# Sliding windows by DMA: one more staged batch, and all direct copies as halves

## The chip, the core and the metric

The kernel runs on one core of a Trainium2 chip. It has no arithmetic at all: it is a program of DMA transfers, which 16 DMA engines carry out. Three of the core's instruction streams issue transfers, and each has a ring (queue) of its own on those engines: SP (SyncE), ACT (ScalarE) and POOL (GpSimd). The metric is the device time of one execution in microseconds (us); lower is better.

## The reference

The input x has 32 batches of 4096 rows of 256 float32. The output holds, for each batch, 127 windows of 64 rows each, which start every 32 rows, so each window shares half of its rows with the next one.

```python
batch, length, dim = (32, 4096, 256)      # window_size 64, stride 32
n_windows = (length - window_size) // stride + 1
for i in range(n_windows):
    start = i * stride
    result[:, i] = x[:, start:start + window_size].copy()
```

A block here is 32 rows of one batch, 32 KB. A batch has 128 blocks (4 MB, 4.19 million bytes); window w is block w followed by block w + 1, 64 KB, and the output of a batch is 8.32 million bytes. All of it is 266 MB.

## The kernel before

There are two ways in which a batch gets to the output.

**Direct.** `Copier.windows` copies n windows from x in HBM to the output in HBM. With `half=None` a row is a whole window of 64 KB (two packets of 32 KB, the largest piece, DIRECT). With `half=0` or `half=1` a row is only the first or the second block of each window (32 KB, one packet), written with a gap of 32 KB, so that two DMAs, a pair, do the same as one full DMA. The usual DMA covers 16 windows (a "sixteen"), one row for each of the 16 engines.

**Staged.** Every third batch (1, 4, 7, ... 31; 11 of them) goes through on-chip memory. `Staging.load` brings the 128 blocks of a batch into a tile of 128 partitions with 32 KB each; `Staging.store` writes the tile out twice, once as the first halves of the windows and once as the second halves. Packets are 16 KB here (IN and OUT). Six tiles are used in turn: `Staging.run` loads six batches, stores six, loads the other five, and stores those. All of this is issued by ACT; before a tile is loaded again, ACT waits for its stores, and before it is stored, for its load. The very first load and the very last store are cut into smaller DMAs. The staged stores write 128 rows although a batch has 127 windows, so each spills one wrong half window into the batch before it (its last window, 126) and one into the batch after it (its window 0). These have to be written again later, after the store.

The direct batches' 127 windows are cut into 7 sixteens, which leaves 15 over: the edges. Beside a staged batch the edges lie at the side of that batch, so that they cover the spilled half window: windows 0 to 14 where the batch before is staged, 112 to 126 where the batch after it is. With two direct batches in each gap between staged ones, each direct batch has one staged neighbour.

**The order.** SP issues the 147 sixteens, batch by batch (the loop from line 174), and one small DMA in the middle for a last half window. For each sixteen a running sum, `share`, decides whether it goes as one full DMA or as a pair of halves: pairs take 90 of 120 while ACT's ring loads, 18 of 120 while it stores, and all of the first 16 turns (and those about the start of the second loads). The counters `first_loads`, `loads` and `stores` estimate from the turns passed which of the two ACT's ring is at. The last but one sixteen counts on the semaphore `near`.

POOL waits for `near` (line 193 on), then issues the edges, batch by batch. Before each it waits until the stores of the staged neighbours are done (`wait_stored`). The edges of all but batch 30, the last direct one, are 20 DMAs of 15 windows; 4 more windows of batch 30 bring them to 304, a multiple of 16. `columns`, also on POOL, brings the next 9 windows of batch 30 in pieces of 4 KB, 16 for each half. SP at last waits for the first stores of tile 31 and then copies the last two windows of batch 30 with `columns`, and waits for everything.

Of the kernel before, what the change touches and what calls it, by code (L numbers as in the profile page):

```python
# [125 lines left out]
@with_exitstack  # L126
def kernel(
    ctx: ExitStack,
    tc: tile.TileContext,
    x: bass.AP,  # L130
    window_size: bass.AP,
    stride: bass.AP,
    out: bass.AP,
):
    nc = tc.nc
    W, S = int(window_size), int(stride)
    B, L, D = x.shape
    n_win = (L - W) // S + 1
    assert out.shape == (B, n_win, W, D)
    c = Copier(x, out, B, L, D, W, S, n_win)  # L140


    staged = [*range(1, B, 3)]
    items = [(b, -1 if b == B - 1 else 0, c.nb) for b in staged]
    place = {b: g for g, (b, _, n) in enumerate(items) if n == c.nb}
    direct = [b for b in range(B) if b not in staged]
    pool = ctx.enter_context(tc.tile_pool(name="xb", bufs=1))
    st = Staging(c, tc, pool, x.dtype, items, 6)
    ring_d, ring_s, ring_r = nc.sync, nc.scalar, nc.gpsimd
    done = tc.alloc_semaphore("done")  # L150
    near = tc.alloc_semaphore("near")
    rest = tc.alloc_semaphore("rest")
    total = {done: 0, near: 0, rest: 0}

    def count(dma, sem):
        dma.then_inc(sem, 16)
        total[sem] += 16

    sixteens = []
    for b in direct:
        w = 15 if b - 1 in staged else 0
        sixteens += [(b, w + 16 * j) for j in range((c.nw - w) // 16)]
    singles = [(B - 1, c.nw - 1, 1)]
    edges = [(b, 0 if b - 1 in staged else 112, 15) for b in direct[:-1]]
    last = B - 2
    edges.append((last, 112, 4))

    first_loads, loads, stores = 6 * 17, 5 * 17, 6 * 34  # L170
    turns = share = 0
    with tc.tile_critical():  # L172
        st.run(ring_s)

        for i, (b, w) in enumerate(sixteens):
            sem = near if i == len(sixteens) - 2 else done
            second = turns - first_loads - stores
            loading = turns < first_loads or 0 <= second < loads
            share += 120 if turns < 16 or -8 <= second < 16 else 90 if loading else 18
            if share >= 120:  # L180
                share -= 120
                turns += 4
                count(c.windows(ring_d, b, w, 16, 0), done)
                count(c.windows(ring_d, b, w, 16, 1), sem)
            else:
                turns += 3
                count(c.windows(ring_d, b, w, 16), sem)
            if i == len(sixteens) // 2:
                for b, w, half in singles:
                    count(c.windows(ring_d, b, w, 1, half, 2048), done)  # L190

        ring_r.wait_ge(near, 16)
        for b, w, n in edges:
            for k in (b - 1, b + 1):
                if k in place and b != last:
                    st.wait_stored(ring_r, place[k])
            count(c.windows(ring_r, b, w, n), rest)


        count(c.columns(ring_r, last, 116, 9), rest)  # L200
        ring_r.drain()  # L201
        st.wait_stored(ring_d, place[B - 1])
        count(c.columns(ring_d, last, 125, 2), done)
        total[st.ended] = st.count[st.ended]
        for sem, n in total.items():
            ring_d.wait_ge(sem, n)
# [35 lines left out]
```

## Time and profile before

| what | us |
|---|---|
| median of 3 runs | 753.65 |
| lowest, highest run | 752.89, 753.98 |
| span of the profiled execution, first to last instruction | 742.1 |
| median of the runs less that span | 11.55 |
| last packet of SP's sixteens ends, from the span's start | 651.4 |
| last packet of ACT's stores ends | 738.9 |
| last packet of POOL's ring ends | 739.7 |

The page gives the span in 40 slices of 18.55 us, with the share of the 16 DMA engines that was busy (in tenths) and what they moved in each. Under it stand the queues: q1 is SP's ring, q10 is ACT's and q0 is POOL's, with packets, MB, and the time of those packets as a share of what 16 engines have in the span. Packets overlap a little, so a share can come out slightly over 1. A DMA's completion is a packet of 4 bytes on each engine that took part. The time between a DMA's issue and its landing is long here (about 100 us on the median for SP's), because many are queued ahead.

### The profile page before, as it was taken

How to read it: one execution, taken by the hardware profiler on the slowest of the kernel's cores; microseconds unless marked ns; L12 is line 12 of the kernel's file. 1: busy time of each engine (PE TensorE's matmuls, PEld its weight loads, DVE VectorE, ACT ScalarE, POOL GpSimd, SP SyncE). 2: the span in 40 equal slices, each digit the busy share in tenths (PEclk: the TensorE clock that was granted, in tenths of full speed). 3: DMA queues.
4: the chain of work that ended last, by engine and by line, in shares of the span. 5: the costliest groups of instructions: out<-in, count | busy, mean ns of one | idle time of the engine just before them, and what ended most of it. 6: DMA issues, size and time to landing. Idle time of an engine off the chain costs nothing.

```text
span 742.1 us, 323 instructions
## 1 busy us (share of the span) xinstructions
POOL 12.7 (2%) x26
## 2 busy tenths in 40 slices
POOL 0000000000000000000000000000000000050100
DMA  8999999999999999999999999999999999999996
GB/s 361 424 430 427 435 431 428 423 435 425 428 427 426 428 428 420 429 435 427 427 427 412 433 435 431 427 436 432 434 424 429 430 424 426 428 435 432 421 420 253
DMA packets 18290, 313.26 MB, mean 422 GB/s; under 512 B 4336, under 2 KB 4336, under 8 KB 4528
## 3 DMA queue, kind: packets, MB, share of 16 engines
q1 hardware_dynamic: 8016, 154.32, 48.8%
q10 hardware_dynamic: 9104, 138.41, 44.0%
q0 software_dynamic: 1168, 20.51, 6.6%
q14 instruction: 2, 0.02, 0.0%
HBM read 220.95 MB, written 267.09 MB: 658 GB/s over the span
## 4 chain that ended last, share of the span: by engine, by line
another core or an unknown queue 92%; POOL 2%; issue 0%; POOLq 0%; SPq 0%
POOL out_dram L34 2%; POOLq L201 0%; POOLq L237 0%; SPq L172 0%; POOLq L114 0%
## 5 line engine op out<-in xcount | busy, mean ns | idle before, releaser
L34 POOL DMA_DIRECT2D out_dram<-in_x_dram x21 | 12.0, 575 | 685.4 <-DMA out_dram<-in_x_dram 648.7
L44 POOL DMA_DIRECT2D out_dram<-in_x_dram x1 | 0.6, 581 | 0.0
L223 POOL MEMSET const-float32-0.0<- 128x1 f32 x1 | 0.1, 98 | 0.2 <-issue 0.2
L223 POOL MEMSET const-bfloat16-1.0<- 128x1 bf16 x1 | 0.1, 101 | 0.0
L223 POOL MEMSET const-float32-1.0<- 128x1 f32 x1 | 0.1, 98 | 0.0
L223 POOL MEMSET const-uint8-127<- 128x1 uint8 x1 | 0.1, 98 | 0.0
## 6 DMA issues: line engine op xcount, KB each, us to landing
out_dram<-in_x_dram SPq DMA_DIRECT2D x92, 1024.0 KB, 99.8
out_dram<-xb ACTq DMA_DIRECT2D x21, 4096.0 KB, 138.5
out_dram<-in_x_dram SPq DMA_DIRECT2D x110, 512.0 KB, 90.2
xb<-in_x_dram ACTq DMA_DIRECT2D x10, 4096.0 KB, 130.5
out_dram<-in_x_dram POOLq DMA_DIRECT2D x20, 960.0 KB, 37.9
xb<-in_x_dram ACTq DMA_DIRECT2D x4, 1024.0 KB, 15.7
out_dram<-xb ACTq DMA_DIRECT2D x2, 1024.0 KB, 110.5
out_dram<-xb ACTq DMA_DIRECT2D x4, 512.0 KB, 94.4
```

Source lines behind the costliest of these rows:

```text
L34: return q.dma_start(out=self.oap((b * self.nw + w0) * 2 + h, [[2 * blk, n], row]), in_=self.xap(b * self.nb + w0 + h, [[blk, n], row]), m ...
L44: return q.dma_start(out=self.oap((b * self.nw + w0) * 2, [[part, 16], [2 * self.blk, n], row]), in_=self.xap(b * self.nb + w0, [[part, 16 ...
L223: nc = _bacc.Bacc("TRN2", target_bir_lowering=False, num_devices=1)
```

## The change

Batches 18 and 20 are staged in place of 19, so that 12 of 32 are staged and three gaps (17, 19, 21) hold one direct batch, with a staged one at either side; the other gaps hold two as before. ACT's ring has two equal groups of six loads and six stores. The edges of a batch with two staged neighbours are cut in two, 7 windows at its start and 8 at its end, and each of the two waits for both neighbours. The number of windows of batch 30 that go with the edges is worked out from their sum (`odd`, 3 here), and `columns` takes the 10 that follow. The running sum with its turns is gone: each sixteen is a pair of halves.

```diff
-    staged = [*range(1, B, 3)]
+    staged = [1, 4, 7, 10, 13, 16, 18, 20, 22, 25, 28, B - 1]
...
-    sixteens = []
+    sixteens, edges = [], []
+    last = B - 2
     for b in direct:
-        w = 15 if b - 1 in staged else 0
-        sixteens += [(b, w + 16 * j) for j in range((c.nw - w) // 16)]
+        first = (15 if b + 1 not in staged else 7) if b - 1 in staged else 0
+        sixteens += [(b, first + 16 * j) for j in range((c.nw - first) // 16)]
+        if b != last:
+            edges += [(b, w, n) for w, n in ((0, first), (first + 112, 15 - first)) if n]
     singles = [(B - 1, c.nw - 1, 1)]
-    edges = [(b, 0 if b - 1 in staged else 112, 15) for b in direct[:-1]]
-    last = B - 2
-    edges.append((last, 112, 4))
-
-    first_loads, loads, stores = 6 * 17, 5 * 17, 6 * 34
-    turns = share = 0
+    odd = -sum(n for _, _, n in edges) % 16
+    edges.append((last, 112, odd))
+
     with tc.tile_critical():
         st.run(ring_s)
 
         for i, (b, w) in enumerate(sixteens):
-            sem = near if i == len(sixteens) - 2 else done
-            second = turns - first_loads - stores
-            loading = turns < first_loads or 0 <= second < loads
-            share += 120 if turns < 16 or -8 <= second < 16 else 90 if loading else 18
-            if share >= 120:
-                share -= 120
-                turns += 4
-                count(c.windows(ring_d, b, w, 16, 0), done)
-                count(c.windows(ring_d, b, w, 16, 1), sem)
-            else:
-                turns += 3
-                count(c.windows(ring_d, b, w, 16), sem)
+            count(c.windows(ring_d, b, w, 16, 0), done)
+            count(c.windows(ring_d, b, w, 16, 1), near if i == len(sixteens) - 2 else done)
...
-        count(c.columns(ring_r, last, 116, 9), rest)
+        count(c.columns(ring_r, last, 112 + odd, 13 - odd), rest)
```

## The prediction

> **What bounds the kernel now.** I read the page's slices first, to see whether the transfers ever pause; then its queue table, for what a byte costs on each ring; then the busy time by stretch; then the waits. No compute engine does anything here, so everything is DMA.
>
> The first view is the page: the span, its 40 slices and the queues.
>
> ```profile
> span 742.1 us, 323 instructions
> ...
> DMA  8999999999999999999999999999999999999996
> GB/s 361 424 430 427 435 431 428 423 435 425 428 427 426 428 428 420 429 435 427 427 427 412 433 435 431 427 436 432 434 424 429 430 424 426 428 435 432 421 420 253
> ...
> q1 hardware_dynamic: 8016, 154.32, 48.8%
> q10 hardware_dynamic: 9104, 138.41, 44.0%
> q0 software_dynamic: 1168, 20.51, 6.6%
> ...
> HBM read 220.95 MB, written 267.09 MB: 658 GB/s over the span
> ```
>
> q1 is SP's ring (direct copies), q10 ACT's (staged loads and stores), q0 POOL's (edges). The three shares add to 99.4% of sixteen engines' span. Only the first and the last slice are not full, so there is no gap to fill: the time is the sum of what the packets cost. The second view gives the rate by stretch (start to end in us, length, POOL busy, clock, DMA share, GB/s).
>
> ```profile
> 0.00:20.00 20.00, 0.20 (x4) 1.00 0.90 367
> 20.00:125.00 105.00, 0.00 (x0) 1.00 1.01 429
> 140.00:400.00 260.00, 0.00 (x0) 1.00 1.00 428
> 420.00:510.00 90.00, 0.00 (x0) 1.00 1.01 433
> 545.00:645.00 100.00, 0.00 (x0) 1.00 1.01 428
> 655.00:735.00 80.00, 6.66 (x12) 1.00 1.00 421
> 735.00:742.00 7.00, 0.00 (x0) 1.00 0.10 40
> ```
>
> The reader sees one ceiling, 428 to 433 GB/s, whether ACT's ring loads (20 to 125, 420 to 510) or stores (140 to 400, 545 to 645). In the trace's packet records the commonest 32 KB direct packet takes 1213 ns and the commonest 16 KB staged packet 611 ns, in every stretch; the means are 1223 and 618 ns, so some packets are drawn out, by 0.8 and 1.1%. A resource that runs against its ceiling in nine tenths of its packets is the engines' own rate. So I ask first how many bytes the change makes them move.
>
> **What the change does to the bytes.** Batch 19 becomes direct, 18 and 20 become staged: 12 staged batches and 20 direct ones. A direct batch moves its 127 windows of 64 KB once, 8.32 MB. A staged one moves 4.19 MB in and twice 4.19 MB out, 138.41 / 11 = 12.58 MB. By ring:
> - q10: 12 x 12.58 = 150.99 MB (+12.58).
> - q1: all 20 direct batches have 7 sixteens (112 windows), 140 in place of 147, each 1.049 MB: 154.32 - 7.34 = 146.98 MB.
> - q0: edges fall from 304 windows to 288 (19 batches x 15, and 3 of batch 30), columns rise from 9 to 10: 298 x 65.5 KB = 19.53 MB (-0.98).
> Together 317.50 MB against 313.24, or +4.26 MB.
>
> Each ring's price comes from its share: q1 0.488 x 742.1 = 362.1 us for 154.32 MB, 2.347 us a MB; q10 326.5 / 138.41 = 2.359; q0 49.0 / 20.51 = 2.388. After: 146.98 x 2.347 = 344.9, 150.99 x 2.359 = 356.2, 19.53 x 2.388 = 46.6; sum 747.7 us against 737.6. **The extra staged batch costs +10.1 us.**
>
> **All direct DMAs as halves.** 92 of 147 sixteens are now full (one DMA of 1 MB); all 140 become pairs of 512 KB. SP issues 280 DMAs of sixteens instead of 202. The data packets stay 32 KB. What grows is one completion packet on each of the 16 engines per DMA, which the packet records show at 9 ns: 78 x 9 ns = 0.7 us, **+0.8 us** with the part that the price per MB had already taken off. The issuing itself is hidden: SP's shortest issue takes 558 ns, 280 of them 156 us in a ring that works over 670 us, and its median DMA lands some 90 to 100 us after its issue, so SP is far ahead. If that lead were gone, each issue would show up at half a microsecond.
>
> A rule speaks against halves here. The Trainium skill, page "DMA: Bandwidth & Descriptors", section "Rules for kernel authors", asks for at least 1 MiB a DMA, and its section "Anatomy of one DMA — SWDGE (gpsimd) path" puts about 2 us fixed on each of POOL's; laid end to end, 78 more DMAs would be an estimated 156 us by that page. The rows above show the engines at share 1.00 in stretches with three quarters halves, so that fixed part lies under other DMAs.
>
> **The pace of the two rings.** The code counts turns: a full is 3 (two packets and a completion), a pair 4, a staged tile 17 (16 packets and a completion), and the engines alternate between rings. The third view, the queues of 545 to 645 us (packets, MB, share), tests it:
>
> ```profile
> q1 hardware_dynamic: 1191, 24.55, 57.7%
> ...
> q10 hardware_dynamic: 1188, 18.22, 43.0%
> ```
>
> As many packets on one ring as on the other. So the order of the end can be forecast. Between them, a pair on q1 and four turns on q10 cost 2 x 1.222 + 4 x 0.576 = 4.75 us, a full and three turns 4.16 us. Before: 92 x 4.16 + 55 x 4.75 = 644 us; the trace ends q1's sixteens at 651.4, 7.5 later (ramp and slow packets). After: 140 x 4.75 + 7.5 = 672 us. Turns on q10: before 10 x 17 + 20 loading, 20 x 17 + 39 storing, 569, so some 71 were left when q1 ended; after 620, less 562, some 60. q0 answers with 69 turns before (38 data packets, 21 + 1 completions, 9 columns) and 70 after (36, 23 + 1, 10). **The two rings still end within 2 or 3 us of each other**, and one ring alone does not starve the engines: from 650 to 655 us, before q0's packets came, nearly all was q10 at 432 GB/s. I cost the new balance at 0, bounds -2 and +3.
>
> **Waits.** The fourth view is what POOL waited for (us, times, longest).
>
> ```profile
> POOL out_dram L34 <- DMA out_dram<-in_x_dram: 648.7, 1, 648.7
> POOL out_dram L34 <- DMA out_dram<-xb: 36.8, 1, 36.8
> ```
>
> The first is `near`, the second the staged store of batch 28, ahead of the edges of 27 and 29. Edges of batches 17, 19 and 21 now come in two (7 and 8 windows), each with waits for both neighbours; tiles 5 to 8 are stored well before 672 us, so these pass at once, for three more issues of 0.57 us on POOL. Again only the edges of 27 and 29 will wait, for batch 28 (21 turns left at 562, about 27 us). Queued behind them on POOL are the 3 windows of batch 30 and the columns. Ahead of them on q0 lie 255 windows, 16.7 MB, which at q0's 246 GB/s (8.62 MB between 660 and 695 us) last 68 us. Cost 0; if that cover were gone, up to 27 us. SP's last wait, for the last tile, stays as it is.
>
> **Slow packets.** The unknown: do 12 tiles and halves everywhere change the drawn-out packets? Stretches with three quarters halves (the code's 90 of 120; 20 to 125 and 400 to 510) average 429.6 GB/s, store stretches with 15% (18 of 120; 140 to 400 and 510 to 645) about 428.1. That is 0.35% of some 485 us of storing (24 stores x 17 turns x 1.187 us), -1.7 us, which I take, since the halved stretches are the nearest rows. Ends: all packets at their commonest time, 0.8% of 362 and 1.1% of 326 us and q0's, -7 us; and the slowest 20 us ahead of the tail, 416 GB/s (400 to 420 us), through all storing, 2.8%, +14 us. The ramp at the start and the thin 7 us at the end are the same code: 0, +-3.
>
> **Sum:** 10.1 + 0.8 - 1.7 = +9.2 us. Profiled span 742.1 + 9.2 = 751.3; the runs' median is 11.5 us above the span (753.65), so **762.8 us**, +1.2%.
>
> **Rivals.**
> - **Slow packets vanish** in storing, as from 420 to 540 us, where 432 GB/s held: 10.9 - 7 = +3.9, 757.6 us. For it: less is read from HBM at a time, as q1's part falls from 57 to about 52%. Against it: in the first loads, with 75% halves, they did not vanish.
> - **HBM decides (faster).** A direct batch reads and writes HBM 16.64 MB, a staged one 12.58: HBM bytes fall by about 4.1 MB. If the 658 GB/s over the span were the limit, that is -6.2 us, 747.5 us. Its condition is that slices with less HBM traffic per byte moved move more. Against it: 140 to 400 us has q1 at 63.48 of 111.19 MB and 428 GB/s, 80 to 120 us q1 at 9.11 of 17.29 and 432: 0.9% apart while HBM traffic differs by 2.9%; and a 32 KB packet cannot fall below the 1213 ns it has when nothing presses. It decides only if the drawn-out share of packet time exceeds the 10.9 us added; it is about 7.
> - **Halves collide in storing.** Both rings would write only every second 32 KB at once. Load stretches with halves have just one such writer. Price half to all of the bound above: 10.9 + 7 to 14, 771.6 to 778.6 us. For it: the edges' last part, 700 to 735, falls to 407 GB/s with other writers mixed. Against: ACT's stores have that pitch already.
> - That the change does not do what it says (the rings end apart) costs little, as shown: inside the forecast's range.
>
> **Chances.** Forecast 0.66 (759.5 to 768), slow packets vanish 0.16 (754 to 759.5), halves collide 0.13, HBM 0.05. A difference under 0.2% (1.5 us) can't be told from none: faster 0.05, same 0.04 (the low end of the second case), slower 0.91. The range leaves out HBM's case, the low edge of the second and most of the third: 756.5 to 768.
>
> **What would show it.** Right: q10 near 151 MB, q1 near 147, engines at 9 to the last slice, mean GB/s again 421 to 425 over a span of 750 to 753, q1's sixteens ending near 672, POOL's second wait under 40 us, commonest packets still 1213 and 611 ns. Wrong: a steady rate of 432 or more in storing (second case), under 422 (third), or a last slice emptier than 253 GB/s (the balance).

## The result, and the profile after

The changed kernel takes 756.38 us (median of 8 runs, 755.60 to 757.53); the kernel before, beside it, 754.11 us (8 runs, 752.89 to 754.59). The ratio is 1.0032, 95% interval 1.0019 to 1.0045: slower by 2.3 us. I had forecast 762.8, with a range from 756.5. The sign was right, the size was four times too large.

One number must be read before the profile. The changed kernel's profiled execution took 756.57 us and its span is 754.8: **only 1.8 us lie outside the span.** The recorded profile of the kernel before spans 742.1, so that execution took about 744 us, while all eight timed runs took 753 to 755. The two spans are 12.7 us apart, the medians 2.3.

The page of the changed kernel: span, the DMA slices, and the queues (packets, MB, share).

```profile
span 754.8 us, 412 instructions
...
DMA  8999999999999999999999999999999999999995
GB/s 359 423 427 429 431 431 431 431 431 430 432 430 432 432 432 431 431 437 431 414 430 429 432 435 431 434 430 431 431 431 426 431 432 433 431 438 424 411 389 178
...
q10 hardware_dynamic: 9920, 151.00, 47.0%
q1 hardware_dynamic: 9040, 146.98, 45.5%
q0 software_dynamic: 1280, 19.53, 6.6%
...
HBM read 216.83 MB, written 267.16 MB: 641 GB/s over the span
```

The bytes are those worked out: 151, 147 and 19.5 MB. The slices are different from those of before: 24 of the 40 stand at 430 to 432, where they had wavered between 412 and 436, and the last three are thinner (178 GB/s in the last, where 253 had been seen before). The same in stretches of the changed kernel (start to end, length, POOL busy, clock, DMA share, GB/s):

```profile
140.00:400.00 260.00, 0.00 (x0) 1.00 1.01 430
520.00:660.00 140.00, 0.00 (x0) 1.00 1.01 431
675.00:735.00 60.00, 4.69 (x9) 1.00 1.01 411
735.00:754.00 19.00, 0.00 (x0) 1.00 0.56 191
```

SP's sixteens end at 669.7 us (672 forecast). ACT's last packet ends at 742.6 us and POOL's at 752.4; before, these two rings ended within a microsecond of each other. From 728 to 742 us POOL's copies are nearly alone (packets, MB, share; 4.83 MB in all, 345 GB/s):

```profile
q0 software_dynamic: 241, 4.56, 94.5%
q10 hardware_dynamic: 26, 0.21, 4.2%
```

POOL's waits:

```profile
POOL out_dram L34 <- DMA out_dram<-in_x_dram: 665.8, 1, 665.8
POOL out_dram L34 <- DMA out_dram<-xb: 20.0, 1, 20.0
```

The second is the wait for batch 28, 20.0 us where 27 was worked out, and the new pairs of waits cost nothing, as forecast.

To compare kernels I use one measure from the packet records, the **drawn-out time**: what each packet took over the commonest time of its size (1213 ns for 32 KB, 611 for 16 KB, 159 for 4 KB), summed and divided by 16 engines. In the recorded trace of before it is 7.6 us, 5.9 of it until SP's sixteens end and 1.7 behind; in the changed kernel's 7.9 us, 2.7 until then and 5.2 behind. POOL's 32 KB packets there average 1320 ns.

### The profile page after: what moved, and what is told of

Its sections match the earlier page's. It is cut to its first block, busy times and chain, and to the rows that moved or that the text cites. A ratio compares the mean times of both kernels' runs of the same rounds, so it can differ in the third digit from the quotient of the medians.

```text
span 754.8 us, 412 instructions
## 1 busy us (share of the span) xinstructions
POOL 13.6 (2%) x28
## 4 chain that ended last, share of the span: by engine, by line
another core or an unknown queue 91%; POOL 1%; issue 0%; POOLq 0%; SPq 0%
POOL out_dram L34 1%; POOLq L191 0%; POOLq L227 0%; SPq L172 0%; POOLq L114 0%
```

## The experiments

Eight runs were made on one chip (the first chip, below), where the kernel before takes 744 us, and three on another (the second), where it takes 754. The record doesn't say on which chip the result itself was measured. The runs are told in an order that makes the argument.

### The kernel before once more, and the changed one (e1, e2)

Both unchanged.

> The kernel before, unchanged, to get a second profile of it. Its recorded profile spans 742.1 us, but the changed kernel's runs are only 1.8 us longer than their span, so a median of 754.1 means that a usual execution of the kernel before spans about 752.3, 10 us more than the one I read. Theory A (slow packets): the 10 us are drawn-out packets; span about 752, mean 32 KB packet on SP's ring 1235 to 1245 ns, mean 16 KB packet on ACT's 625 to 632 ns, commonest still 1213 and 611. Theory B (the end): span about 752, packet means as recorded (1223 and 618 ns), and the last 40 us emptier by 10 us. Theory C: the recorded profile is usual, span 742 again, and the time around the span differs.

Measured: 744.04 us, beside 744.33 us in 13 other runs of the same kernel; span 742.2; 32 KB packets 1223.4 ns, 16 KB 617.6 ns, drawn-out time 7.6 us. The recorded profile is usual for this chip (theory C as to the span). But the time around the span doesn't differ, it is 1.8 us here too. So the recorded profile of before came from an execution like those on this chip, and the timed runs from somewhere 10 us slower.

> The changed kernel, unchanged, for a second profile beside e1 on the same chip. Theory A and B alike: 756 us, span 754 to 756, mean 32 KB packet on SP's ring 1214 to 1220 ns, and the end (after SP's sixteens) again loses 10 us or more to slow POOL packets and engines that have run out. If the means move by over 10 ns here too, slow packets are a matter of the execution and not of the halves.

Measured: 754.09 us against 744.33, ratio 1.0132 (1.0117 to 1.0147), +9.8 us; span 752.7; 32 KB packets 1216.2 ns, 16 KB 614.2. On a chip where the kernel before runs as in the recorded trace, **the change costs 9.8 us; 9.2 had been worked out from that trace.** The packets' time, divided by 16, sums to 747.1 us against 737.2 in e1: 9.9 us, nearly all of the difference. The packet mean is as expected; the time is 2 us under the 756 expected. The changed kernel takes 754 here and 756.4 on the chip of the result; the kernel before 744 and 754. What has to be found is why the old one loses 10 us where the new one loses 2.

### What draws packets out: form or memory (e5, e10)

```diff
-        st.run(ring_s)
-            count(c.windows(ring_d, b, w, 16, 0), done)
-            count(c.windows(ring_d, b, w, 16, 1), near if i == len(sixteens) - 2 else done)
+            if i < 70:
+                count(c.windows(ring_d, b, w, 16, 0), done)
+                count(c.windows(ring_d, b, w, 16, 1), done)
+            else:
+                count(c.windows(ring_d, b, w, 16), done)
...
-        (edges, columns and their waits)
```

> The staged batches, the edges and the columns are left out: SP's ring copies the 140 sixteens of the changed kernel alone, the first 70 as pairs of halves and the last 70 as full DMAs, so every byte moved is read from and written to HBM. Theory A' (memory ceiling): packets are drawn out where HBM traffic passes some 650 to 680 GB/s; moving at 431 GB/s would need 862, so SP alone reaches only 325 to 350 GB/s, 32 KB packets 1490 to 1600 ns at a busy share of 1.0, halves and fulls within 2%. Theory F (form): it is the shape of the full DMAs, two overlapping 64 KB rows, that draws packets out; then halves run near 1213 ns and 431 GB/s, and fulls slower.

Measured: 445.99 us, 32 KB packets 1562 ns on average. The rate in stretches, halves first, then fulls:

```profile
20.00:200.00 180.00, 0.00 (x0) 1.00 1.00 334
250.00:430.00 180.00, 0.00 (x0) 1.00 1.00 333
```

Both forms run at the same rate, so the form of the full DMA is not the cause here. The engines are busy throughout (share 1.00) with packets of 1.56 us in place of 1.21: something other than their own rate holds them. Each byte is read and written, so this is 2 x 334 = 668 GB/s of HBM traffic, which I read as **a ceiling of memory traffic beside the engines' 432 GB/s.** By itself e5 does not exclude a limit of one ring of copies; e3, below, speaks against it: three rings meet the same figure, and there the staged packets are drawn out too.

The queues from 140 to 400 us, while ACT's ring stores, first before, then changed:

```profile
DMA packets 6176, 111.19 MB, mean 428 GB/s; under 512 B 1312, under 2 KB 1312, under 8 KB 1328
...
q1 hardware_dynamic: 3088, 63.48, 57.4%
```

```profile
DMA packets 7060, 111.91 MB, mean 430 GB/s; under 512 B 1970, under 2 KB 1970, under 8 KB 1986
...
q1 hardware_dynamic: 3532, 57.51, 51.7%
```

Each byte moved is read or written in HBM, and q1's direct ones are both. Before, that is (111.19 + 63.48) / 260 = 672 GB/s: in storing it runs at about this ceiling. The changed kernel has (111.91 + 57.51) / 260 = 652 GB/s, and is under it.

The Trainium skill, page "HBM Reference", section "Specifications (TRN2)", gives about 716 GB/s for the memory that two cores share. Direct copies alone, from one core, reached 668 here, so that figure would have put the ceiling too high to matter.

> As e5: SP's ring alone copies the 140 sixteens; staged batches, edges and columns are left out. Where the kernel before takes 744 us: 446 us and 334 GB/s again. Where it takes 754 us, the theory of a ceiling that differs from chip to chip wants 2% or more less, 455 us or longer; if it is 446 there too, the 10 us are not the memory's rate.

This run fell on the second chip, whose 13 runs of the kernel before have a median of 753.77 us. Measured: 453.33 us, 1.6% longer than e5, packets 1586 ns.

```profile
20.00:200.00 180.00, 0.00 (x0) 1.00 1.00 327
250.00:430.00 180.00, 0.00 (x0) 1.00 1.00 329
```

About 328 GB/s, 656 GB/s of traffic: lower on this chip by 1.8%, from one run on each. The expectation asked for 455 us and 2%, so this is a little short of it, but in the direction and of the order that the theory wants: 656 is further under what the kernel before asks for in storing (432 x 1.57 = 678), and still above the 652 of the changed one.

### The kernel before where it is slow (e8, e11)

> The kernel before, unchanged, beside e5 to e7: its median was 754.1 us where the change was measured and 744.3 us in e1. Theory A' with a ceiling that differs from chip to chip: where its runs take about 754 us, the 32 KB mean in storing is 1245 ns or more and e5's rate is 2% or more lower than where they take 744 us.

It fell on the first chip again: 744.47 us, 32 KB packets 1225.4 ns. Its drawn-out time is 9.2 us where e1 has 7.6, so traces of one kernel on one chip differ by 1.6 us in this measure.

> The kernel before, unchanged, for a trace of an execution of 754 us if this chip gives one. Ceiling theory: then 32 KB packets in storing mean 1245 ns or more, at an unchanged end. Where it takes 744 us: a repeat of e1, packets 1223 ns.

On the second chip: 750.85 us (one run, 3 us under that chip's median), span 749.1. 32 KB packets on SP's ring average 1237.8 ns and 16 KB ones 626.0, against 1223.4 and 617.6 in e1; the commonest are 1213 and 611 as ever, which is theory A of e1. The storing stretches of e11, which stood at 428 in the recorded trace:

```profile
140.00:400.00 260.00, 0.00 (x0) 1.00 1.01 422
545.00:645.00 100.00, 0.00 (x0) 1.00 1.00 420
```

The drawn-out time is 16.7 us, against 7.6 in e1: 9.1 us more, where the span is 6.9 longer. HBM traffic between 140 and 400 us is (109.73 + 62.69) / 260 = 663 GB/s, down from 672. The extra time of this execution is drawn-out packets, most of them in the two-ring part (14.4 us until the sixteens end, 6.0 in e1). In storing alone the 32 KB mean is 1243.7 ns (1224.8 in e1), just under the 1245 expected for a run of 754. Why this chip has the lower ceiling is not known.

### One part of the change at a time (e3, e4)

e3: 11 staged batches, and all sixteens as pairs.

```diff
-            sem = near if i == len(sixteens) - 2 else done
+            sem = near if i == 124 else done
...
-            share += 120 if turns < 16 or -8 <= second < 16 else 90 if loading else 18
+            share += 120
```

> The kernel before with 11 staged batches, but every sixteen as a pair; SP's ring then has 590 turns against 569 of ACT's, so the edges are let go after sixteen 124 instead of the last but one, so that POOL's ring does not run alone. Theory A: slow packets vanish while two rings run (1214 to 1218 ns), so engine time falls to 730 to 733 us and the run takes 737 to 744 us, 1.3 to 2.2% under the kernel before. Theory B: packets as before, only the end differs: 750 to 756 us. If halves do nothing: 754 to 758.

Measured: 755.36 us, ratio 1.0153 (1.0138 to 1.0168) to 744.33: slower by 11 us, which no theory had said (their figures that come near it were reckoned from a kernel before of 754 us). The trace splits it. Stretches of e3 with two rings, then with three:

```profile
140.00:340.00 200.00, 0.00 (x0) 1.00 1.00 431
605.00:705.00 100.00, 5.54 (x10) 1.00 1.00 389
```

With two rings the halves hold 431 GB/s, as theory A said. With SP, POOL and ACT together it is 389; the queues of e3 from 605 to 705 us:

```profile
q0 software_dynamic: 754, 15.30, 39.5%
q1 hardware_dynamic: 752, 12.55, 32.1%
q10 hardware_dynamic: 753, 11.04, 28.7%
```

Three rings alternate packet by packet, so two thirds of the turns are direct. (38.90 moved + 27.85 direct) / 100 us = 667 GB/s of traffic, the ceiling of e5 again. The 16 KB staged packets take 681 ns there in place of 611 and the 32 KB ones 1341, so it isn't the copies alone that wait. With 11 staged batches halves only put the direct bytes off to the end, where they cost more: the drawn-out time is 18.2 us.

e4: 12 staged batches with the old running sum, `loads` set to 6 x 17.

```diff
-            count(c.windows(ring_d, b, w, 16, 0), done)
-            count(c.windows(ring_d, b, w, 16, 1), near if i == len(sixteens) - 2 else done)
+            share += 120 if turns < 16 or -8 <= second < 16 else 90 if loading else 18
+            if share >= 120: (a pair, turns += 4)
+            else: (a full DMA, turns += 3)
```

> 12 staged batches as in the changed kernel, but the sixteens full or halved by the old running sum (its second loads set to 6 x 17 turns). SP's ring ends some 145 turns before ACT's. Theory A: slow packets come back in storing (SP's 32 KB mean 1230 ns or more), the run takes 761 to 768 us. Theory B: steady part as in the changed kernel; the edges end long before the stores, ACT's ring alone fills the engines to the end, 748 to 754 us.

Measured: 756.02 us, ratio 1.0157 (1.0124 to 1.0191). 32 KB packets on SP's ring are back at 1227.5 ns (1232.1 in storing, as theory A asked), 16 KB ones at 620.3, drawn-out time 10.4 us against 6.6 in e2. So the mix, not the number of staged batches, draws the packets out. The total lies between the theories, 1.9 us over the changed kernel, with intervals that overlap: what the packets lose shows only in part in the time.

### Tries to do better (e6, e7, e9)

e6: the pairs of before spread evenly (`share += 45` in the line that e3 changes).

> The kernel before with its 55 pairs spread evenly (45 of 120 at every sixteen) in place of 90 in loading and 18 in storing; same bytes, same number of DMAs, same end. Direct bytes are then about 55.7% of all while two rings run, between the 53% and the 57.4% of before. Theory A': the storing part drops under the ceiling, its 32 KB mean falls from 1223 to 1214 to 1218 ns, the run is 2 to 5 us under the kernel before. Theory G (ACT's stores draw packets out whatever the mix): no change, within 1.5 us.

Measured: 743.85 us, ratio 0.9996 (0.9984 to 1.0008) to 743.88, the median of 13 further runs of the kernel before: no change, theory A' wrong as to the gain. The first two stretches of e6 load and store in the first group, the others in the second:

```profile
20.00:140.00 120.00, 0.00 (x0) 1.00 1.00 421
140.00:260.00 120.00, 0.00 (x0) 1.00 1.01 432
420.00:520.00 100.00, 0.00 (x0) 1.00 1.01 423
520.00:640.00 120.00, 0.00 (x0) 1.00 1.01 432
```

Storing came clear, as said, though 92 of the 147 sixteens are still full, so neither there is the form the cause. Loading, which had been nearly clear with its 53% of direct bytes, slowed down. The drawn-out time went from 7.6 (e1) to 9.4 us. Traffic was 656 GB/s in the first loads, drawn out, and 672 in the first stores, clear. So the ceiling is not one number, and the 668 of e5 only marks its region: with loads in the mix it bites at a smaller direct part than with stores. Why is not shown.

e7: the changed kernel, its edges let go two sixteens earlier (`len(sixteens) - 4`).

> The changed kernel with the edges let go two sixteens earlier (9.5 us), so that POOL's ring starts before SP's ends and is less alone at the end, where it moved 290 to 350 GB/s. Theory A': the last 20 us fill up, 2 to 5 us less than the changed kernel (749 to 752 where that takes 754). If three rings at a time cost as much as POOL alone: no change, within 1 us.

Measured: 754.29 us, ratio 1.0138 (1.0123 to 1.0153); the changed kernel beside e1 took 754.09. No change, the expectation's second case: POOL's 32 KB packets fall from 1311 (e2) to 1263 ns, and those of SP and ACT rise.

e9: the changed kernel with 31 of its 140 sixteens full (`share += 94`, a pair when 120 is reached), so that ACT's ring outlasts POOL's.

> 12 staged batches as in the changed kernel, with 31 of the 140 sixteens full, spread evenly (94 of 120). SP's ring then has 529 turns and ends some 30 turns earlier, so that POOL's ring ends before ACT's and is never alone, while direct bytes stay at 53% of all, under the ceiling. Ceiling theory: the thin last 30 us (282 GB/s from 720 to 752 us) close by 5 to 9 us, steady packets stay at 1213 ns: 745 to 749 us where the kernel before takes 744 and the changed one 754. If the end is thin for another reason (engines out of step): 752 to 756. On a chip where the kernel before takes 754: 747 to 752, faster than both.

Measured, on the second chip: 756.21 us, ratio 1.0030 (1.0014 to 1.0047) to 753.77. It beats neither. POOL's packets are at 1240 ns, its ring ends before ACT's, and still the end is thin (stretches of e9: storing, loading, the edges, the last):

```profile
140.00:350.00 210.00, 0.00 (x0) 1.00 1.01 431
420.00:520.00 100.00, 0.00 (x0) 1.00 1.00 426
660.00:740.00 80.00, 6.42 (x12) 1.00 1.00 422
740.00:754.90 14.90, 0.00 (x0) 1.00 0.44 176
```

So the thin end is not POOL's being alone, and the time is nearest the expectation's second case, engines out of step. The records don't say which engine a packet ran on, but they do show how many packets run at once: 16 until 744 us, and one at a time from 748 to 753 us, of all three rings in turn (share 0.06, a sixteenth). That is what one engine out of step, with packets of every ring still to move, looks like; why it came last is not shown. No version tried beats the kernel before.

## Why the prediction was right or wrong

**The engines' bytes: right.** +4.26 MB, priced at +10.9 us with the completions. The packets' sums of e2 and e1 differ by 9.9 us, the medians by 9.8, with 1.0 us less drawn out.

**SP's lead, the new waits and POOL's cover: right,** all at zero. The half-sized DMAs kept 431 GB/s. The 156 us for 78 more DMAs took POOL's price for DMAs that SP issues; no run shows such a price.

**The pace of the rings: right for SP, wrong for the end.** SP's sixteens ended at 669.7 us, 672 forecast. (A full and three turns come to 4.17 us by the prediction's own terms, not 4.16, which makes the forecast 671. Its stretch from 650 to 655 us holds 23% of POOL's packets; ACT's ring was alone, at 432 GB/s, only from 651.5 to 653.7.) But "the two rings still end within 2 or 3 us of each other" failed: they ended 9.8 us apart. The forecast's own counts, some 60 turns left for ACT and 70 for POOL, already lay ten apart; by the packet records each engine had 50 packets of ACT's ring and 80 of POOL's to go (66 and 73 before). So POOL's copies were left alone, and a direct copy alone is held by the memory ceiling: from 728 to 742 us they moved 345 GB/s, 674 GB/s of traffic. The drawn-out time behind the sixteens is 5.2 us in the changed kernel against 1.7 in the recorded trace of before, 3.5 more (2.9 between e1 and e2). The price was 0 with a bound of +3, and the forecast's sign for a wrong balance, a last slice emptier than 253 GB/s, came true with 178.

**The step that failed is the slow packets, and the last line of the sum hid it:** "the runs' median is 11.5 us above the span". I took a difference between two executions for a fixed time around one. As a base it did no harm, since 753.65 is what the kernel before takes there. But the runs show about 1.8 us around the span, so some 10 us of the median lay inside executions that I had not seen, and I priced the slow packets, -1.7 us with -7 as the most that could vanish, from a quicker execution with 7.6 us of them. As e11 and e10 show, the missing time is drawn-out packets in a place with a lower memory ceiling.

**What the term measured.** Where an execution of the kernel before holds 16.7 us (e11) and the changed one 7.9 (the recorded trace of the result), the change takes away 8.8 us: 10.9 - 8.8 = +2.1, and +2.3 was measured. On the first chip it takes away 7.6 - 6.6 = 1.0: 10.9 - 1.0 = +9.9, and +9.8 was measured. In both places it is a gain and a loss: until SP's sixteens end the drawn-out time falls from 14.4 to 2.7 us (6.0 to 2.1 on the first chip), and behind them it grows from 2.3 to 5.2 (1.5 to 4.5). That the forecast of +9.2 met the first chip's +9.8 is thus partly luck: the gain was larger than -1.7, and the loss at the end had been put at nothing.

That 2.1 lies so near to 2.3 is luck too. The spans of the two executions are 5.7 us apart, and the packets make up 2.1 of that; the rest is time in which engines had nothing to move (span less the packets' sum: 6.4 us in the result's trace, 2.7 in e11; 5.6 in e2 and 5.0 in e1). And e11 is a single execution, 3 us quicker than its chip's median. So the relief of some 9 us is known to about 3. That the chip of the result is like the second one is inferred from its 754 us for the kernel before: no trace of before was taken there, and the changed kernel was not run on the second chip.

**The rivals.** "Slow packets vanish" named the mechanism, and its band of 754 to 759.5 us holds the measured 756.38; but its price came from one quick execution, and it left out the loss at the end. Storing ran at 430 to 431 GB/s, just under its sign of 432. "HBM decides" was half right: there is a ceiling, at 668 and 656 GB/s. I had dismissed it because 428 and 432 GB/s differ by less than the traffic; e5 shows what that overlooked, that the kernel before sits where both ceilings meet. Its deciding point held: faster only if more than 10.9 us of packet time were drawn out and went away; by these traces 8.8 did. "Halves collide" fell: halves in storing ran at 431.

## What to carry to other kernels

Take the time outside the span from a run that shows both. And when the profile's span and the timed runs are far apart, don't call the gap overhead: the profile may be of a quicker execution, and the gap may be the very thing that the change acts on. A mix of copies within HBM and transfers through on-chip memory met two ceilings here, bytes moved by the engines and bytes read and written in HBM. The mix that sat where they meet lost 10 us from one place to another (744 to 754), the one below lost 2 (754 to 756). Measure the second ceiling by running one kind alone, before pricing a change of the mix, and expect it to move with the share of loads and stores. And when a change moves work between rings, count what each has left when the first one ends.

## What the runs showed of the hardware

- One core's HBM traffic in direct copies alone is 668 GB/s on one chip and 656 on another (packets 1562 and 1586 ns at a busy share of 1.0), while two rings, one of them staged, hold 431 GB/s moved on both. With loads in the mix packets were drawn out at 656 GB/s of traffic, with stores they were clear at 672 (e6).
- The same program took 744 us on one chip (26 runs, 742.11 to 746.27) and 754 on another (13 runs, 752.43 to 755.01).
- Rings alternate packet by packet, whatever a packet's size, completions included: 754, 752 and 753 packets from three rings in 100 us (e3).
